# Batch norm on one core: loads cut into two transfers of 64 partitions, stores held until half of the next load has landed, and an added DRAIN on GpSimd

## The chip, the core and the metric

The kernel runs on one core of a Trainium2 chip. Time is device microseconds of one execution, from several executions of each kernel; less is better. A profile is one further execution, taken by the hardware profiler, with its own time. The engines that matter here are ScalarE (ACT in the profile), VectorE (DVE), GpSimd (POOL) and SyncE (SP), and 16 DMA engines that move bytes between the main memory (HBM) and the on-chip memory (SBUF, 128 partitions).

## What is computed

Batch normalization with given statistics: every element of `x` (32 x 256 x 128 x 128, float32, 537 MB) is scaled and shifted by two numbers that depend only on its channel.

```python
mean, var = running_mean.reshape(1, -1, 1, 1), running_var.reshape(1, -1, 1, 1)
return gamma * (x - mean) / np.sqrt(var + 1e-5) + beta
```

The output is as large as the input, so each execution reads 537 MB and writes 537 MB.

## The kernel before

The input is seen as 64 tiles (image, half of the channels), each of 128 channels on 128 partitions by 16384 elements, which is 64 KB a partition and 8 MB a tile. Three buffers of this size (`bufs`, `NBUF = 3`) take turns: tile i lies in buffer i mod 3, is loaded, changed in place and stored from there.

**Parameters.** Four small loads (L92), a transpose and a few small instructions on VectorE (L109 to L125) make `scale_t` and `shift_t`, one column for each half of the channels. This is over at 17 us.

**Loads** are issued by SP on one DMA queue. Tile 0 comes in two halves of the columns (L89 and L96), with the four small loads between them; tiles 1 and 2 as one DMA each (L98); tiles 3 to 63 as one DMA of 128 partitions each (L160), which waits on the semaphore `stored` of its buffer, that is, for the store of the tile three before. When a load has landed, its semaphore (`first` for tiles 0 to 2, `loaded` after that) has risen by 16. The helper `landed(i)` (L100) gives semaphore and value for tile i.

**Computing.** For each tile ScalarE does one ACTIVATE in place (L142, `scale * x + shift`) as soon as `landed(i)` holds. VectorE takes a part of the first and of the last tile (L131), which shortens these two. ScalarE counts its tiles in `adone`.

**Stores.** Tiles 0 to 60 are stored by GpSimd (L172), each as one DMA that waits for `adone`; the last three by ScalarE itself, in the order of its own instructions. So loads, GpSimd's stores and ScalarE's stores have a DMA queue each, and all run on the same 16 DMA engines.

**The end.** SP waits for the last stores (L177, L178). Then the block that holds the hand-written part closes (its instructions are at L73): every engine executes a DRAIN, an instruction that waits until the engine's earlier work is done, and SP waits for all of them.

Of the kernel before, what the change touches and what calls it, by code (L numbers as in the profile page):

```python
# [8 lines left out]
NBUF = 3  # L9
PAD = 936  # L10
NHEAD = 3
NTAIL = 3
# [4 lines left out]
@with_exitstack  # L17
def kernel(
    ctx: ExitStack,
    tc: tile.TileContext,  # L20
    x: bass.AP,
    gamma: bass.AP,
    beta: bass.AP,
    running_mean: bass.AP,
    running_var: bass.AP,
    out: bass.AP,
):
    nc = tc.nc
    eps = 1e-5
    f32 = mybir.dt.float32  # L30

    N, C, H, W = x.shape
    P = nc.NUM_PARTITIONS
    assert C % P == 0
    NCB = C // P
    HW = H * W
    NT = N * NCB
    B = 32
    NQ = P // B
    NE = 16  # L40
    NPAR = 4

    xr = x.rearrange("n (cb p) h w -> (n cb) p (h w)", p=P)
    outr = out.rearrange("n (cb p) h w -> (n cb) p (h w)", p=P)

    params = ctx.enter_context(tc.tile_pool(name="params", bufs=1))
    data = ctx.enter_context(tc.tile_pool(name="data", bufs=1))
    params.tile([P, PAD], f32, name="pad", tag="pad")
    bufs = [data.tile([P, HW], f32, name=f"t{s}", tag=f"t{s}") for s in range(NBUF)]
    rows = params.tile([B, NPAR * C], f32, name="rows", tag="rows")  # L50
    turned = params.tile([B, NPAR * C], f32, name="turned", tag="turned")
    par = params.tile([P, NPAR, NCB], f32, name="par", tag="par")
    eps_t = params.tile([P, 1], f32, name="eps_t", tag="eps")
    std_t = params.tile([P, NCB], f32, name="std_t", tag="std")
    rstd_t = params.tile([P, NCB], f32, name="rstd_t", tag="rstd")
    scale_t = params.tile([P, NCB], f32, name="scale_t", tag="scale")
    ms_t = params.tile([P, NCB], f32, name="ms_t", tag="ms")
    shift_t = params.tile([P, NCB], f32, name="shift_t", tag="shift")

    loaded = [tc.alloc_semaphore(f"loaded{s}") for s in range(NBUF)]
    stored = [tc.alloc_semaphore(f"stored{s}") for s in range(NBUF)]
    closed = [tc.alloc_semaphore(f"closed{s}") for s in range(NBUF)]
    early = tc.alloc_semaphore("early")
    first = [tc.alloc_semaphore(f"first{s}") for s in range(NHEAD)]
    vdone = tc.alloc_semaphore("vdone")
    adone = tc.alloc_semaphore("adone")
    fetched = tc.alloc_semaphore("fetched")
    vec = tc.alloc_semaphore("vec")  # L70
    act = tc.alloc_semaphore("act")

    with tc.tile_critical():  # L73
        count = [0]

        def step(inst, sem=None, value=None):
            if sem is not None:
                inst._wait_ge(sem, value)
            elif count[0]:
                inst._wait_ge(vec, count[0])  # L80
            inst.then_inc(vec, 1)
            count[0] += 1
            return count[0]

        left, right = slice(0, HW // 2), slice(HW // 2, HW)
        last = NT - 1


        nc.sync.dma_start(out=bufs[0][:, left], in_=xr[0][:, left]).then_inc(early, 16)  # L89
        zeroed = step(nc.vector.memset(rows[:], 0.0))  # L90
        for r, ap in enumerate((running_var, gamma, beta, running_mean)):
            inst = nc.sync.dma_start(out=rows[0:NE, r * C : (r + 1) * C], in_=ap.partition_broadcast(NE))  # L92
            if r == 0:
                inst._wait_ge(vec, zeroed)
            inst.then_inc(fetched, 16)
        nc.sync.dma_start(out=bufs[0][:, right], in_=xr[0][:, right]).then_inc(first[0], 16)  # L96
        for i in range(1, NHEAD):
            nc.sync.dma_start(out=bufs[i][:], in_=xr[i]).then_inc(first[i], 16)  # L98

        def landed(i):  # L100
            if i < NHEAD:
                return first[i], 16
            s = i % NBUF
            before = 1 if s < NHEAD else 0
            return loaded[s], 16 * (i // NBUF + 1 - before)


        step(nc.vector.memset(eps_t[:], eps))  # L108
        step(nc.vector.transpose(out=turned[:], in_=rows[:]), fetched, 16 * NPAR)  # L109
        blocks = turned.rearrange("p (rc q b) -> p rc q b", q=NQ, b=B)  # L110
        flat = par.rearrange("p r cb -> p (r cb)")
        for q in range(NQ):
            placed = step(nc.vector.tensor_copy(out=flat[q * B : (q + 1) * B], in_=blocks[:, :, q, 0]))  # L113
        var_t, gamma_t, beta_t, mean_t = (par[:, r] for r in range(NPAR))
        nc.scalar.activation(  # L115
            out=std_t[:],
            in_=var_t,
            func=mybir.ActivationFunctionType.Sqrt,
            bias=eps_t[:],
            scale=1.0,  # L120
        )._wait_ge(vec, placed).then_inc(act, 1)
        step(nc.vector.reciprocal(out=rstd_t[:], in_=std_t[:]), act, 1)  # L122
        step(nc.vector.tensor_mul(out=scale_t[:], in0=gamma_t, in1=rstd_t[:]))  # L123
        step(nc.vector.tensor_mul(out=ms_t[:], in0=mean_t, in1=scale_t[:]))  # L124
        ready = step(nc.vector.tensor_sub(out=shift_t[:], in0=beta_t, in1=ms_t[:]))  # L125
        nc.vector.wait_ge(vec, ready)
        nc.scalar.wait_ge(vec, ready)

        def vector_part(i, first_col, end):
            t, cb = bufs[i % NBUF], i % NCB  # L130
            return nc.vector.tensor_scalar(  # L131
                out=t[:, first_col:end],
                in0=t[:, first_col:end],
                scalar1=scale_t[:, cb : cb + 1],
                scalar2=shift_t[:, cb : cb + 1],
                op0=mybir.AluOpType.mult,
                op1=mybir.AluOpType.add,
            ).then_inc(vdone, 1)

        def scalar_part(i, first_col):  # L140
            t, cb = bufs[i % NBUF], i % NCB
            return nc.scalar.activation(  # L142
                out=t[:, first_col:],
                in_=t[:, first_col:],
                func=mybir.ActivationFunctionType.Identity,
                bias=shift_t[:, cb : cb + 1],
                scale=scale_t[:, cb : cb + 1],
            ).then_inc(adone, 1)


        def share(i):
            return VHEAD if i == 0 else VLAST if i == last else 0

        vector_part(0, 0, HW // 2)._wait_ge(early, 16)
        vector_part(last, 0, VLAST)._wait_ge(*landed(last))


        for i in range(NHEAD, NT):
            s = i % NBUF
            inst = nc.sync.dma_start(out=bufs[s][:], in_=xr[i])  # L160
            if i >= NBUF:
                inst._wait_ge(stored[s], 16 * (i // NBUF))
            inst.then_inc(loaded[s], 16)

        for i in range(NT):
            eng = nc.gpsimd if i < NT - NTAIL else nc.scalar
            packet = {"single_packet": True} if i < NT - NTAIL else {}
            written = (stored if i < NT - NTAIL else closed)[i % NBUF]
            scalar_part(i, share(i))._wait_ge(*landed(i))
            if i in (0, last):  # L170
                eng.wait_ge(vdone, 1 if i == 0 else 2)
            eng.dma_start(out=outr[i], in_=bufs[i % NBUF][:], **packet)._wait_ge(adone, i + 1).then_inc(  # L172
                written, 16
            )

        for s in range(NBUF):
            nc.sync.wait_ge(stored[s], 16 * ((NT - NTAIL - s + NBUF - 1) // NBUF))  # L177
            nc.sync.wait_ge(closed[s], 16)  # L178
# [30 lines left out]
```

## Time and profile before

| | |
|---|---|
| Time, median of 3 runs | 2497.66 us (2485.99 to 2506.67) |
| Profiled execution, time | 2486.73 us |
| Its span | 2485.0 us |
| ScalarE busy | 885.6 us (36%) |
| VectorE busy | 13.1 us (1%) |
| GpSimd busy | 32.7 us (1%) |
| Read from and written to HBM | 536.94 MB, 536.87 MB |
| Mean rate over the span | 432 GB/s |
| One full-tile ACTIVATE | 14.04 us |
| Idle of ScalarE that a load ended | 1555.7 us |
| Wait of SP for stores, before its loads | 2370.4 us, 61 times |

The span runs from the first to the last instruction of the profiled execution; its time is 1.7 us longer. In the rows of the profile, L142 is a line of the kernel, an arrow `out<-in` names what an instruction writes and reads, and what stands in brackets or behind "idle before" is how long the engine had waited and for what. SPq, POOLq and the like are the sequencers of the engines, which wait, issue DMAs and execute DRAINs.

### The profile page before, as it was taken

The page shows a single profiled execution, that of the slowest core. Times are in us where ns is not written, and L with a number is a line of the kernel's source. Part 1 is how long each engine was busy: PE and PEld are TensorE (multiplying, and loading weights), DVE is VectorE, ACT ScalarE, POOL GpSimd, SP SyncE. Part 2 cuts the span into 40 slices and gives each one's busy share as a digit, 9 for nine tenths or more (in the row PEclk, how much of TensorE's full clock was granted, in tenths as well). Part 3 has the DMA queues.
Part 4 walks back from the last instruction along what each step waited for, and adds up shares of the span by engine and source line. Part 5 has one row for each costly group of instructions (what it writes and reads, how often), then busy time and mean ns, then how long its engine had stood idle before and what let it go on. Part 6 is the DMA issues. An engine that isn't in the chain of part 4 may idle for free.

```text
span 2485.0 us, 274 instructions
## 1 busy us (share of the span) xinstructions
DVE 13.1 (1%) x13; ACT 885.6 (36%) x66; POOL 32.7 (1%) x65
## 2 busy tenths in 40 slices
DVE  1000000000000000000000000000000000000000
ACT  2342432423424334243342433424324244243331
POOL 0000000000000000000000000000000000000000
DMA  9999999999999999999999999999999999999998
GB/s 414 431 439 438 423 439 438 436 426 439 438 427 435 438 439 423 439 438 435 427 439 438 426 436 438 438 424 439 438 434 428 439 438 425 437 438 437 425 439 371
DMA packets 18707, 1073.84 MB, mean 432 GB/s; under 512 B 2128, under 2 KB 2192, under 8 KB 2192
## 3 DMA queue, kind: packets, MB, share of 16 engines
q1 hardware_dynamic: 9488, 536.94, 49.9%
q0 software_dynamic: 8784, 511.71, 47.5%
q10 hardware_dynamic: 432, 25.17, 2.3%
q14 instruction: 3, 0.02, 0.0%
HBM read 536.94 MB, written 536.87 MB: 432 GB/s over the span
## 4 chain that ended last, share of the span: by engine, by line
another core or an unknown queue 61%; ACT 35%; DMA 2%; issue 0%; SPq 0%; DVE 0%; ACTq 0%; DVEq 0%
ACT t L142 35%; DMA t<-in_x_dram 2%; SPq L92 0%; DVE rows L90 0%; ACTq L172 0%; SPq L96 0%; DVE eps_t L108 0%; DVEq L204 0%; SPq L73 0%
## 5 line engine op out<-in xcount | busy, mean ns | idle before, releaser
L142 ACT ACTIVATE t<-t,shift_t,scale_t 128x16384 f32<-128x16384 f32 (+1 forms) x64 | 884.0, 13813 | 1555.7 <-DMA t<-in_x_dram 1555.7
L172 POOL DMA_DIRECT2D out_dram<-t x61 | 32.5, 533 | 2314.5 <-ACT t L142 2314.5
L131 DVE TENSOR_SCALAR t<-t,scale_t,shift_t 128x8192 f32<-128x8192 f32 (+1 forms) x2 | 9.6, 4812 | 2428.0 <-DMA t<-in_x_dram 2427.9
L115 ACT ACTIVATE std_t<-par,eps_t 128x2 f32<-128x2 f32 x1 | 0.3, 295 | 13.9 <-DVE par L113 13.9
L115 ACT ACT_TABLE_LOAD x1 | 1.3, 1283 | 0.9 <-SPq L73 0.9
L109 DVE STREAM_TRANSPOSE turned<-rows 32x1024 f32<-32x1024 f32 x1 | 1.2, 1232 | 11.8 <-DMA rows<-in_running_mean_dram 11.8
L90 DVE MEMSET rows<- 32x1024 f32 x1 | 0.9, 912 | 1.2 <-SPq L73 1.2
L113 DVE COPY par<-turned 32x8 f32<-32x8 f32 x4 | 0.6, 162 | 0.1
L122 DVE RECIPROCAL rstd_t<-std_t 128x2 f32<-128x2 f32 x1 | 0.2, 166 | 0.4 <-ACT std_t L115 0.4
L124 DVE TENSOR_TENSOR ms_t<-par,scale_t 128x2 f32<-128x2 f32 x1 | 0.2, 161 | 0.0
L125 DVE TENSOR_TENSOR shift_t<-par,ms_t 128x2 f32<-128x2 f32 x1 | 0.2, 161 | 0.0
L123 DVE TENSOR_TENSOR scale_t<-par,rstd_t 128x2 f32<-128x2 f32 x1 | 0.2, 160 | 0.0
L193 POOL MEMSET const-float32-0.0<- 128x1 f32 x1 | 0.1, 98 | 0.2 <-issue 0.2
L193 POOL MEMSET const-bfloat16-1.0<- 128x1 bf16 x1 | 0.1, 101 | 0.0
L193 POOL MEMSET const-float32-1.0<- 128x1 f32 x1 | 0.1, 98 | 0.0
L193 POOL MEMSET const-uint8-127<- 128x1 uint8 x1 | 0.1, 98 | 0.0
L108 DVE MEMSET eps_t<- 128x1 f32 x1 | 0.1, 59 | 0.1
## 6 DMA issues: line engine op xcount, KB each, us to landing
t<-in_x_dram SPq DMA_DIRECT2D x2, 4096.0 KB, 15.9
t<-in_x_dram SPq DMA_DIRECT2D x63, 54.6
out_dram<-t POOLq DMA_DIRECT2D x61, 46.9
out_dram<-t ACTq DMA_DIRECT2D x3, 32.9
rows<-in_running_var_dram SPq DMA_DIRECT2D x1, 16.0 KB, 11.1
rows<-in_gamma_dram SPq DMA_DIRECT2D x1, 16.0 KB, 10.9
rows<-in_beta_dram SPq DMA_DIRECT2D x1, 16.0 KB, 10.7
rows<-in_running_mean_dram SPq DMA_DIRECT2D x1, 16.0 KB, 10.6
```

Source lines behind the costliest of these rows:

```text
L90: zeroed = step(nc.vector.memset(rows[:], 0.0))
L109: step(nc.vector.transpose(out=turned[:], in_=rows[:]), fetched, 16 * NPAR)
L113: placed = step(nc.vector.tensor_copy(out=flat[q * B : (q + 1) * B], in_=blocks[:, :, q, 0]))
L115: nc.scalar.activation(out=std_t[:], in_=var_t, func=mybir.ActivationFunctionType.Sqrt, bias=eps_t[:], scale=1.0,)._wait_ge(vec, placed).t ...
L122: step(nc.vector.reciprocal(out=rstd_t[:], in_=std_t[:]), act, 1)
L123: step(nc.vector.tensor_mul(out=scale_t[:], in0=gamma_t, in1=rstd_t[:]))
L124: step(nc.vector.tensor_mul(out=ms_t[:], in0=mean_t, in1=scale_t[:]))
L125: ready = step(nc.vector.tensor_sub(out=shift_t[:], in0=beta_t, in1=ms_t[:]))
L131: return nc.vector.tensor_scalar(out=t[:, first_col:end], in0=t[:, first_col:end], scalar1=scale_t[:, cb : cb + 1], scalar2=shift_t[:, cb ...
L142: return nc.scalar.activation(out=t[:, first_col:], in_=t[:, first_col:], func=mybir.ActivationFunctionType.Identity, bias=shift_t[:, cb : ...
L172: eng.dma_start(out=outr[i], in_=bufs[i % NBUF][:], **packet)._wait_ge(adone, i + 1).then_inc(written, 16)
L193: nc = _bacc.Bacc("TRN2", target_bir_lowering=False, num_devices=1)
```

## The change

Three things are changed.

1. From tile 1 on, a load is two DMAs, partitions 0 to 63 and partitions 64 to 127, issued by SP one after the other on the same queue. The first raises a new semaphore `lower` of its buffer, the second raises `loaded`. Only the first waits for the store three tiles before. Tile 0 is loaded as before. ScalarE and VectorE wait for both semaphores before they read a tile.
2. The store of tile i (i < 63) waits, besides `adone`, until the lower half of tile i + 1 has landed. This holds for GpSimd's stores and for ScalarE's stores of tiles 61 and 62, where the wait stands in ScalarE's own order.
3. After its last store GpSimd waits until its stores have landed, and then executes a DRAIN.

```diff
-    first = [tc.alloc_semaphore(f"first{s}") for s in range(NHEAD)]
+    lower = [tc.alloc_semaphore(f"lower{s}") for s in range(NBUF)]
+    first = tc.alloc_semaphore("first")
...
+        half = P // 2
+
+        def load(i):
+            s = i % NBUF
+            inst = nc.sync.dma_start(out=bufs[s][:half], in_=xr[i][:half])
+            if i >= NBUF:
+                inst._wait_ge(stored[s], 16 * (i // NBUF))
+            inst.then_inc(lower[s], 16)
+            nc.sync.dma_start(out=bufs[s][half:], in_=xr[i][half:]).then_inc(loaded[s], 16)
+
+        def landed(i):
+            if i == 0:
+                return first, 16
+            s = i % NBUF
+            return loaded[s], 16 * (i // NBUF + (1 if s else 0))
+
+        def half_landed(i):
+            s = i % NBUF
+            return lower[s], 16 * (i // NBUF + (1 if s else 0))
+
         for i in range(1, NHEAD):
-            nc.sync.dma_start(out=bufs[i][:], in_=xr[i]).then_inc(first[i], 16)
+            load(i)
...
         vector_part(0, 0, HW // 2)._wait_ge(early, 16)
+        nc.vector.wait_ge(*half_landed(last))
         vector_part(last, 0, VLAST)._wait_ge(*landed(last))
 
         for i in range(NHEAD, NT):
-            s = i % NBUF
-            inst = nc.sync.dma_start(out=bufs[s][:], in_=xr[i])
-            if i >= NBUF:
-                inst._wait_ge(stored[s], 16 * (i // NBUF))
-            inst.then_inc(loaded[s], 16)
+            load(i)
 
         for i in range(NT):
...
+            if i:
+                nc.scalar.wait_ge(*half_landed(i))
             scalar_part(i, share(i))._wait_ge(*landed(i))
+            if i < last:
+                eng.wait_ge(*half_landed(i + 1))
             if i in (0, last):
                 eng.wait_ge(vdone, 1 if i == 0 else 2)
             eng.dma_start(out=outr[i], in_=bufs[i % NBUF][:], **packet)._wait_ge(adone, i + 1).then_inc(
                 written, 16
             )
+
+        for s in range(NBUF):
+            nc.gpsimd.wait_ge(stored[s], 16 * ((NT - NTAIL - s + NBUF - 1) // NBUF))
+        nc.gpsimd.drain()
```

## The prediction

> **What bounds the kernel now.** I read the page first, then two stretches of the span with the busy share of the DMA engines, then the timeline of one tile, then the waits of SP, then the end. The page's DMA queues (packets, MB, share of the time of 16 engines):
>
> ```profile
> span 2485.0 us, 274 instructions
> ...
> q1 hardware_dynamic: 9488, 536.94, 49.9%
> q0 software_dynamic: 8784, 511.71, 47.5%
> q10 hardware_dynamic: 432, 25.17, 2.3%
> ```
>
> Loads (q1) and stores (q0 from GpSimd, q10 from ScalarE) together hold the 16 engines for 49.9 + 47.5 + 2.3 = 99.7% of the span, 2477.5 us of 2485.0. ScalarE is busy 36%. Two stretches, one tile in the middle and the last 9 us (after the length: busy DVE, ACT and POOL, the clock, DMA share, GB/s):
>
> ```profile
> 207.50:246.10 38.60, 0.00 (x0) 14.04 (x1) 0.53 (x1) 1.00 1.00 435
> 2476.00:2485.00 9.00, 0.00 (x0) 0.00 (x0) 0.00 (x0) 1.00 0.00 1
> ```
>
> In the middle no DMA time is free; from about 2476 on the DMA does nothing. The timeline of that tile:
>
> ```profile
> 207.50 14.04 ACT L142 ACTIVATE t<-t,shift_t,scale_t 128x16384 f32<-128x16384 f32 x1 [24.57 <-DMA t<-in_x_dram]
> 221.84 0.53 POOL L172 DMA_DIRECT2D out_dram<-t  x1 [38.08 <-ACT t L142]
> 230.00 0.33 SPq L160 DMA_DIRECT2D t<-in_x_dram  x1
> 246.28 14.04 ACT L142 ACTIVATE t<-t,shift_t,scale_t 128x16384 f32<-128x16384 f32 x1 [24.74 <-DMA t<-in_x_dram]
> ```
>
> Call the landing of a tile T (207.5). Its store is issued at T+14.3. The store before it lands at T+22.5, since that releases the load at 230.00. The next tile lands at T+38.6 to T+38.8. So the store queue is handed new work 8.2 us before it is empty, the load queue 16.3 us before. A tile is 128 rows of 64 KB each way, 8 rows an engine if they are spread evenly; 16 rows in 38.63 us is 2.414 us a row (27.1 GB/s an engine). Issue to landing, from the page:
>
> ```profile
> t<-in_x_dram SPq DMA_DIRECT2D x63, 54.6
> out_dram<-t POOLq DMA_DIRECT2D x61, 46.9
> ```
>
> 54.6 = 16.3 in the queue + 38.3; 46.9 = 8.2 + 38.7: a load and a store run side by side, each at half the rate. The end, from SP's waits and from the instructions of the kernel's closing (duration in ns: least, median, most):
>
> ```profile
> SPq L73 <- POOLq L73: 4.5, 1, 4.5
> ```
> ```profile
> L73 POOLq DRAIN  x1: 5047/5047/5047, 2479.0 to 2479.0; - x1
> ```
> ```profile
> L204 POOLq DRAIN  x3: 34/34/108, 2484.1 to 2484.7; - x3
> ```
>
> After the last byte SP waits 4.5 us more for one DRAIN of GpSimd that takes 5.05 us. Three others, with no DMA issued since the one before, take 0.03 to 0.11 us.
>
> **Halves.** 63 loads become 126, each of 64 rows. Bytes and row length stay. SP issues 63 more at 0.33 us, 20.8 us in all, on an engine that waits 2370 us for stores; the second issue of a pair goes out 0.4 us after the first, under 16.3 us of queued work: nothing. Two of the extra issues stand at the start (tiles 1 and 2), ahead of loads that wait for stores until 75 us: nothing. Each transfer posts 16 more completions of 4 bytes, 63 an engine; in the trace's packet records one takes 9 ns, so +0.6 us if none is hidden. The rows are the unknown. No transfer of the trace goes to 64 partitions. One bound is a row as now, 2.414 us; the other is two engines that write to the same part of SBUF and halve each other, 4.83 us. The nearest row in size and path, the full-tile load, is the first, and I take it; the other bound is a rival below.
>
> **The hold.** Store i now also waits for the lower half of tile i+1. With halves served one after the other that half lands at T+19.3 (half of 38.6), and ScalarE is done at T+14.04, so the store goes out at about T+19.7 instead of T+14.3: 5.4 us of the store queue's 8.2 are used, 2.8 are left. The store lands at most 5.4 us later, the load that it releases too, and that queue's cover falls from 16.3 to 10.9 us. Should the store queue run dry for a row, its engines go on with load rows at the same rate (early in the span, with loads alone, the queue moved bytes without stores too), and the row lost by one queue is won by the other. Cost 0 while either queue has rows; behind the waiting store on GpSimd stands only the next store. If both covers were gone, each tile would show a gap; that is a rival too. ScalarE's extra wait before each ACTIVATE is for a half that landed earlier: some tens of ns, in an engine with 24.6 us idle a tile.
>
> **The tail.** The last three stores stand on ScalarE, where a hold also delays the next ACTIVATE. Tile 62's activation starts at 2412.42; its store would wait until about 2412.4 + 19.3 = 2431.7 instead of going at 2426.49. The next ACTIVATE waits for its load (2449.76) anyway: nothing. The delayed store leaves more rows for the time in which the last tile is computed (2449.76 to 2456.15), when only store rows can feed the DMA. In the records the store of tile 62 lands at 2459.4, so that cover is thin now, some 3 us, and gets wider. In this profile it just suffices, so nothing is won here.
>
> **The DRAIN.** GpSimd's last store lands at 2396.4 (records). Then 5.05 us of DRAIN run beside 76 us of other traffic. If the closing DRAIN then costs what the three short ones cost, SP's 4.5 us go. Bounds: 4.5 won, or 0 if that DRAIN is long whenever GpSimd has issued DMAs, or for another reason. I take 4.5, by the three rows. What is late next is nothing: the other engines' arrivals at 2479.0.
>
> **Sum.** On the profiled execution, 2486.73: −4.5 + 0.6 + 0 = 2482.8. That execution is 10.9 us under the median of the three runs (2485.99 to 2506.67), whose excess no trace shows. A thin tail cover could be a part of it, and that part the hold would take. I leave half of the 10.9: 2488. This case alone ranges from 2478 (another 4.8 less) to 2510 (the DRAIN wins nothing and 20 us of spread as above).
>
> **Rivals.** *Collisions in the half tile (slower).* All 16 engines work on 64 partitions at a time. That few partitions do get all 16 engines the counts bear out: q1's 9488 packets are 8384 rows and pieces of rows and 69 × 16 completions, the 16-partition parameter loads with 16 too. If 64 partitions take in only half of 434 GB/s, 217 GB/s, a load row that coincides with its partner's takes 2.41 us more. Per tile an engine has 8 load rows; each that collides adds 2.41 × 64 = 154 us. It decides the sign from 0.3 rows a tile on (40 us); one is 2637, all eight 3718. For it: the engines' rows of a kind now run nearly in step, as the DMA bursts show. Against: loads need only 217 GB/s beside stores, so partners that alternate, one loading while the other stores, never collide, and an engine ahead by half a tile writes to the other half. The trace cannot settle it; 0.32, half of it under three rows a tile. [...]
>
> *The hold empties the queues (slower).* If the two halves share the engines, the lower lands with the upper at T+38.6 and the store goes out 24 us later than now. Both covers are gone: load i+2 and store i run together, end together, and the next load waits for the store's completion and its issue. Completion (DMA idle from about 2477, SP released at 2478.8) and first bytes after an issue (0.96 to about 2) are 2.5 us a tile; 61 of them are 153 us: 2636. For it: both halves stand on one queue at once. Against: one queue is served in order, as the 16.3 us of queueing show. 0.07. [...]
>
> *The DRAIN isn't shortened:* its closing copy waits as long. 2487 on the profiled execution, up to 2498. 0.07.
>
> *Faster by over 1%.* The DMA floor of 2477.5 and the ends leave 7 us; only if the before runs sit high (2507) and the hold steadies all of them at 2480 is it 1%. 0.04.
>
> **How the numbers follow.** Forecast 0.50. About 1% is what a measurement of this kernel tells from no change: 2472.7 to 2522.6. Within: 0.50 + 0.07 = 0.57; slower 0.32 + 0.07 = 0.39; faster 0.04. The range takes 2478 to 2510 (0.56 with the DRAIN rival), the empty queues (0.07) and collisions up to 2.7 rows a tile, 2482.8 + 2.7 × 154 = 2900 (0.16): 0.79.
>
> **What would show it.** Right: DMA share 1.00 in the middle, ACT landings still 38.6 us apart, GpSimd's issue near T+19.7, SP's closing wait near zero with a long GpSimd DRAIN near 2400. Collisions: DMA share 1.00 at a lower GB/s. Empty queues: share under 1.00 and landings 41 us apart. My forecast is wrong if the rate in the middle falls under 430 GB/s.

## The result, and the profile after

The changed kernel takes 3434.7 us (median of 5 runs, 3403.74 to 3455.42) against 2497.66 us before (with two runs more 2485.99 to 2520.68): 1.372 times the time, with a 95% interval of 1.364 to 1.380. The ratio is of the fast runs alone and leaves out the one of 3455.42 us, more than 1.5% above the fastest. The profiled execution took 3446.63 us, its span is 3444.9 us. The page's DMA queues (packets, MB, share of the time of 16 engines):

```profile
span 3444.9 us, 465 instructions
...
q1 hardware_dynamic: 10496, 536.94, 61.2%
q0 software_dynamic: 8784, 511.71, 36.3%
q10 hardware_dynamic: 432, 25.17, 1.7%
```

The bytes are the same, and the 16 engines are still busy 99.2% of a span that is 960 us longer. So the engines hardly wait more than before; the same rows take longer. In engine time, share times span: loads 2108 us (before 1240), stores 1309 us (before 1237), idle 28 us (before 7). The added 960 us are 868 in loads, 72 in stores and 20 in idle time. Two tiles, from landing to landing (length, busy DVE, ACT and POOL, clock, DMA share, GB/s):

```profile
1009.30:1112.93 103.63, 0.00 (x0) 28.08 (x2) 1.06 (x2) 1.00 1.00 325
```

DMA share 1.00 at 325 GB/s, where 435 GB/s went with the same share before: the sign that the prediction had named for collisions. The timeline of one tile:

```profile
1009.30 14.04 ACT L159 ACTIVATE t<-t,shift_t,scale_t 128x16384 f32<-128x16384 f32 x1 [39.11 <-DMA t<-in_x_dram]
1036.92 0.53 POOL L190 DMA_DIRECT2D out_dram<-t  x1 [50.07 <-DMA t<-in_x_dram]
1043.85 0.47 SPq L104 DMA_DIRECT2D t<-in_x_dram  x1
1044.36 1.35 SPq L108 DMA_DIRECT2D t<-in_x_dram  x1
1059.32 14.04 ACT L159 ACTIVATE t<-t,shift_t,scale_t 128x16384 f32<-128x16384 f32 x1 [35.97 <-DMA t<-in_x_dram]
```

A tile lands at 1009.30 and the next one 50.0 us later (38.6 before). GpSimd's store is released by the load's half, at T+27.6, not by ScalarE, which was done at T+14.04. The load issued at 1043.85 stands behind a load that lands at 1059.32, so the load queue is still handed work 15.5 us before it is empty. The store queue is not always so well covered. One tile earlier:

```profile
986.32 0.53 POOL L190 DMA_DIRECT2D out_dram<-t  x1 [55.11 <-DMA t<-in_x_dram]
986.33 0.47 SPq L104 DMA_DIRECT2D t<-in_x_dram  x1
```

The load at 986.33 was released by the landing of the store before, so the store at 986.32 found its queue empty. In the trace as a whole, 19 of the 60 stores that GpSimd issues after its first one go out less than 1 us before the store ahead of them lands, or after it; in the kernel before, all 60 go out at least 7.7 us ahead. The load queue has at least 6.7 us of work left at each issue. Issue to landing:

```profile
t<-in_x_dram SPq DMA_DIRECT2D x126, 63.7
out_dram<-t POOLq DMA_DIRECT2D x61, 57.5
```

In the records of single rows (64 KB, one engine), a load row has a mean of 4.14 us, a tenth of them under 2.84 and a tenth over 5.04; before, nearly all took 2.418. A store row has a mean of 2.56 us (before 2.418). The more load rows run at once, the longer they take: 3.44 us where some 8 of the 16 engines hold one while the row runs, 4.44 us at some 12 and 5.01 us at some 16. In the kernel before it is 2.42 to 2.43 us at all these counts.

The DRAIN did what was forecast. Of the closing instructions, the one of GpSimd is now

```profile
L74 POOLq DRAIN  x1: 34/34/34, 3443.7 to 3443.7; - x1
```

34 ns in place of 5047, and SP no longer waits for it. The added DRAIN has the 5047 ns now, 100 us ahead of the end, beside the last loads and stores:

```profile
L197 POOLq DRAIN  x1: 5047/5047/5047, 3342.3 to 3342.3; - x1
```

GpSimd's last store had landed before it, as in the kernel before (2396.4, the DRAIN at 2479.0), so no trace shows what the 5047 ns go into.

### The profile page after: what moved, and what is told of

It is laid out like the page before. It is cut to its first block, busy times and chain, and to the rows that moved or that the text cites. A ratio compares the mean times of both kernels' runs of the same rounds, so it can differ in the third digit from the quotient of the medians.

```text
span 3444.9 us, 465 instructions
## 1 busy us (share of the span) xinstructions
DVE 13.1 (0%) x13; ACT 885.6 (26%) x66; POOL 32.7 (1%) x65
## 4 chain that ended last, share of the span: by engine, by line
another core or an unknown queue 92%; DMA 4%; SPq 3%; ACT 0%; issue 0%; DVE 0%; ACTq 0%; DVEq 0%; POOLq 0%
DMA t<-in_x_dram 3%; SPq L108 2%; DMA out_dram<-t 1%; SPq L104 1%; ACT t L159 0%; SPq L93 0%; DVE rows L91 0%; SPq L97 0%; ACTq L190 0%; DVE eps_t L125 0%; DVEq L227 0%; ACTq L184 0%; ACTq L187 0%; POOLq L187 0%
## 6 DMA issues: line engine op xcount, KB each, us to landing
rows<-in_beta_dram SPq DMA_DIRECT2D x1, 16.0 KB, 10.9
```

## The experiments

**Moving data alone.** The first question was what a row costs when 64 partitions are loaded. This kernel issues loads, then stores, then both, in stretches with a wait between them. The first three stretches:

```diff
+        for k in range(9):
+            load(k % 3, slice(0, 128))
+        settle(nc.sync)
+        for k in range(9):
+            load(k % 3, slice(0, 64))
+        settle(nc.sync)
+        for k in range(9):
+            load(k % 3, slice(32, 96))
+        settle(nc.sync)
...
```

> Moves data only, in stretches one after the other: nothing is computed and only a part of the output is written. Nine loads each of partitions 0 to 127, 0 to 63, 32 to 95, 64 to 127, 0 to 31; then six stores each of 0 to 127, 0 to 63, 32 to 95; then eight loads of 32 to 95 beside four full stores, and eight loads of 0 to 63 beside four full stores. Theory (64 partitions on one side take half the rate): loads at 434, 217, 434, 217 and 217 GB/s, a row of 64 KB in 2.41 us where the group lies on both sides and 4.83 us where it lies on one; beside stores, loads of 32 to 95 keep 2.42 us a row and loads of 0 to 63 don't. Rival (fewer than 128 partitions are slow whichever they are): 32 to 95 as slow as 0 to 63. Stores: the trace of the kernels says nothing; as the loads if the limit holds for reads too, 434 GB/s in all three if it holds for writes only.

One window inside each stretch, in this order: loads of 0 to 127, of 0 to 63, of 32 to 95; stores of 0 to 127, of 0 to 63; loads of 32 to 95 and then of 0 to 63, both beside full stores (length, busy POOL, clock, DMA share, GB/s):

```profile
20.00:160.00 140.00, 0.00 (x0) 1.00 0.99 429
200.00:340.00 140.00, 0.00 (x0) 1.00 0.99 202
376.00:440.00 64.00, 0.00 (x0) 1.00 1.02 440
...
760.00:840.00 80.00, 1.06 (x2) 1.00 1.00 433
870.00:960.00 90.00, 1.62 (x3) 1.00 1.02 210
...
1060.00:1200.00 140.00, 1.60 (x3) 1.00 1.01 413
1240.00:1380.00 140.00, 1.06 (x2) 1.00 1.00 301
```

The DMA engines are equally busy in all of them (share 0.99 to 1.02), and the rate falls by half where the 64 partitions are 0 to 63 (202 GB/s of 429). It does not fall for 32 to 95 (440), a transfer of the same shape, size and number of rows. From the records, over whole stretches:

```
                    GB/s   row us           GB/s   row us
loads  0 to 127     431    2.43     stores  431    2.43
loads  0 to 63      204    5.12     stores  204    5.11
loads  32 to 95     429    2.43     stores  430    2.43
loads  64 to 127    204    5.12
loads  0 to 31      204    5.12
```

So it is not the number of partitions but which they are. 0 to 31 are as fast as 0 to 63 (204 GB/s both), and 32 to 95, with 32 partitions from either side of 64, have the full rate (429). Loads and stores are alike in the groups that both moved (204 and 204, 429 and 430). The theory holds for these groups, except that a row of a group on one side takes 5.12 us, somewhat more than twice 2.42 (4.84). Beside full stores, the loads of 0 to 63 have 4.36 us a row and the stores 2.55: nearly the 4.14 and 2.56 of the changed kernel. Beside full stores, the loads of 32 to 95 have 2.64 us in the mean and 2.42 in the median, so most of them are as short as undisturbed ones, but not all.

**The hold taken away.** This leaves the half-tile loads alone, with the DRAIN.

```diff
-            if i < last:
-                eng.wait_ge(*half_landed(i + 1))
```

> The changed kernel without the hold: stores wait for the ACTIVATE alone. Theory (collisions): stays at 3350 to 3500 us, load rows still about 4.1 us in the mean. Rival (the hold empties the queues): within 2% of the kernel before, about 2490 us.

It took 3282.8 us in one run, with load rows of 3.84 us. The halves carry the loss without the hold. The time lies below the expected range, and below all runs of the changed kernel, so the hold seems to cost time there too, some 164 us between the two profiled executions, as far as a single run can say. The DMA share stayed at 1.00, so with the hold rows are longer:

```profile
1000.00:1200.00 200.00, 0.00 (x0) 56.16 (x4) 2.13 (x4) 1.00 1.00 332
```

The traces show a part of the reason. Without the hold, 3 of the 60 stores found the store queue empty or within 1 us of it, with the hold 19. While store rows are missing, more engines hold load rows at once: fourteen or more for 17% of the time with the hold, 11% without. Even at equal counts rows are longer with the hold (3.44 us against 3.15 at some 8), so the rest stays open.

**Other partitions in the first transfer.** The same kernel cut so that the first transfer of a tile lies on both sides.

```diff
-            inst = nc.sync.dma_start(out=bufs[s][:half], in_=xr[i][:half])
+            inst = nc.sync.dma_start(out=bufs[s][32:96], in_=xr[i][32:96])
...
-            nc.sync.dma_start(out=bufs[s][half:], in_=xr[i][half:]).then_inc(loaded[s], 16)
+            nc.sync.dma_start(out=bufs[s][0:32], in_=xr[i][0:32]).then_inc(loaded[s], 16)
+            nc.sync.dma_start(out=bufs[s][96:128], in_=xr[i][96:128]).then_inc(loaded[s], 16)
...
```

> The changed kernel with the loads cut at other partitions: first 32 to 95, then 0 to 31, then 96 to 127, so three transfers a tile. Theory (a group of partitions that lies in both outer quarters' sides of SBUF gets the full rate, 0 to 63 alone or 64 to 127 alone half of it): 4 of 8 rows an engine don't collide; in the changed kernel 8 rows lost 1.72 us each, so 4 x 1.72 x 64 = 440 us over 2482: 2850 to 3000 us. Rival (a transfer of fewer than 128 partitions is slow whichever they are, or each transfer costs): 3440 us or more, since there are more and smaller transfers.

It took 3325.4 us in one run: faster than any run of the changed kernel although it has a transfer more, but outside both expectations. The records show why the size was off. The load rows of each tile, in order of their start, in eight groups of sixteen (mean us, means over 63 tiles):

```
middle first:    3.38  2.66  2.60  3.05 | 4.78  4.85  4.71  4.43
changed kernel:  3.92  3.98  4.02  3.59 | 4.03  4.53  4.81  4.26
```

The first four groups are mostly rows of 32 to 95, and the median of the second to fourth is 2.42 us: free, as the theory says. The other four, rows of the two outer quarters, lose more than the 1.72 us that I had carried over from the changed kernel: with 4.69 us in the mean they are not far from the 5.12 us of loads that run alone. That fits the store queue, which was empty or within 1 us of it at 38 of the 60 stores here; the engines were also idle for 2.6% of the span, which the expectation had not counted. I take the first and the fourth group to hold rows of two kinds, since they stand where the kinds change and their means (3.38 and 3.05) lie between those of the groups on either side: an estimate.

**Stores cut at 64 as well.**

```diff
...
-            eng.dma_start(out=outr[i], in_=bufs[i % NBUF][:], **packet)._wait_ge(adone, i + 1).then_inc(
-                written, 16
-            )
+            eng.dma_start(out=outr[i][:half], in_=bufs[i % NBUF][:half], **packet)._wait_ge(
+                adone, i + 1
+            ).then_inc(written, 16)
+            eng.dma_start(out=outr[i][half:], in_=bufs[i % NBUF][half:], **packet).then_inc(written, 16)
...
```

> The changed kernel with its stores cut at partition 64 too. Theory (64 partitions on one side take half the rate, reads like writes, as the stores of the data-only run did): store rows now stretch like the load rows, from 2.56 us to about 4.1; 8 x 1.6 x 64 = 820 us more, 4000 to 4600 us. Rival (only writes into SBUF collide in a mixed stream): about 3450 us as before this edit.

It took 3579.9 us in one run: between the two. ScalarE's three stores, the last of which runs alone, have 3.73 us a row (2.46 in the changed kernel), GpSimd's 2.73 (2.56). So store rows of one side do take longer, but in the mixed stream little (0.17 us). One might think that the engines, mostly in long load rows, rarely hold store rows together. The records do not bear that out: GpSimd's rows have 2.68 us where some 8 engines hold one and still only 2.89 us at some 14. The reason stays open.

**Halves of the columns.** Everything of the change is kept but the cut: two transfers of 128 partitions by half a row.

```diff
-            inst = nc.sync.dma_start(out=bufs[s][:half], in_=xr[i][:half])
+            inst = nc.sync.dma_start(out=bufs[s][:, left], in_=xr[i][:, left])
...
-            nc.sync.dma_start(out=bufs[s][half:], in_=xr[i][half:]).then_inc(loaded[s], 16)
+            nc.sync.dma_start(out=bufs[s][:, right], in_=xr[i][:, right]).then_inc(loaded[s], 16)
```

> Everything of the changed kernel stays (two transfers a load, the hold, the DRAIN), but the two transfers are halves of the columns on all 128 partitions (rows of 32 KB) instead of halves of the partitions. Theory (engines collide on the part of SBUF that 64 partitions cover): collisions go, about 434 GB/s in the middle, 2480 to 2500 us. Rival (two transfers a load, or the hold, cost the time): stays above 3000 us.

It took 2596.4 us (6 runs, 2578.4 to 2599.7), 1.039 times the kernel before (1.033 to 1.046). That lies outside both expectations, and far nearer the first: by the medians, the cut at partition 64 is 838 of the 937 us lost. But the column halves are not free either. Its page:

```profile
span 2597.9 us, 465 instructions
...
q1 hardware_dynamic: 18560, 536.94, 49.9%
q0 software_dynamic: 8784, 511.71, 47.5%
```

The shares of the queues are those of the kernel before to the digit, in a span 4.5% longer: again longer rows (a load row of 32 KB 1.265 us in the mean where 1.213 is the undisturbed one, a store row 2.525), though no transfer here lies on one side alone. And the store queue runs dry:

```profile
1001.41 0.33 SPq L102 DMA_DIRECT2D t<-in_x_dram  x1
1001.78 0.53 POOL L188 DMA_DIRECT2D out_dram<-t  x1 [39.34 <-DMA t<-in_x_dram]
```

The load was released by the landing of the store before, so the next store goes out some 0.4 us too late; at all 60 stores it is 0.3 to 6.5 us. Three further kernels and a second data-only one followed this second effect.

> The column halves (rows of 32 KB) without the hold. The column kernel with the hold was 4% slower than the kernel before, its rows 4% longer at a DMA share of 1.00. Theory A (rows of unequal length take the load and store turns of the engines out of step, and out of step they stretch): still 2570 to 2610 us. Theory B (the hold does it): 2480 to 2510 us.

Without the hold: 2566.8 us, 1.027 times the kernel before (1.022 to 1.033), just under the range of theory A. Not the hold, then, or not it alone. The store queue is still empty at 30 of the 60 stores.

> The column halves with the hold, and each store also as two transfers of half the columns, so that rows of loads and stores are equally long again (32 KB). Theory A (unequal rows): back to 2480 to 2520 us. Theory B (the hold): stays at 2570 to 2610 us.

With the stores cut by columns as well (two DMAs a store, edited as above but with `left` and `right`): 2487.57 us, and 0.9966 times the kernel before (0.9934 to 0.9997). All ten runs lie within 2487.18 to 2488.31, those of the kernel before on the same chip within 2485.59 to 2520.69. That agrees with theory A as written, but the next run speaks against its mechanism.

> Moves data only, in stretches: nothing is computed and only a part of the output is written. Ten loads beside ten stores each time, with no wait but for the buffers: full rows of both; loads by halves of the columns beside full stores; both by halves of the columns; loads and stores of partitions 32 to 95; then the column loads alone. Theory A (unequal rows): rows 2.42 us (1.21 for half a row) everywhere but in the second stretch, there about 4% more. Rival (loads of 32 KB rows are longer by themselves): the third and the last stretch stretch too.

Windows of its five stretches: full rows both ways, column loads beside full stores, column halves both ways, partitions 32 to 95 both ways, column loads alone:

```profile
60.00:380.00 320.00, 0.00 (x0) 1.00 1.00 432
440.00:680.00 240.00, 0.00 (x0) 1.00 1.01 436
850.00:1160.00 310.00, 0.00 (x0) 1.00 1.00 434
1230.00:1370.00 140.00, 0.00 (x0) 1.00 1.00 432
1420.00:1560.00 140.00, 0.00 (x0) 1.00 1.00 430
```

No stretch loses, the unequal one neither (its rows have 1.225 and 2.418 us). Unequal rows alone stretch nothing here, with both queues kept full. So theory A falls as it was stated. What the second stretch does show is that the stores alone moved 291 of its 436 GB/s, two thirds, which fits rows that take turns, one of 64 KB beside one of 32 KB. In the two kernels with unequal rows the stores may so run ahead until their queue is dry, as counted above; where both are cut it never is (9.1 us of work left at a store read in the kernel with the hold, at least 7.8 us at each store without it). That the dry queue costs the time there is a rival that no run here excludes. It can't be all, as the next run shows.

> Loads and stores by halves of the columns and the DRAIN, without the hold. With the hold all ten runs lay within 2487.2 to 2488.3 us, the runs of the kernel before within 2485.6 to 2520.7. If the hold steadies the runs: spread of more than 10 us again, median 2485 to 2500. If the equal rows do it alone: within 2 us again, at 2483 to 2488 us.

Column halves both ways but no hold: 2552.1 us, 1.021 times (1.016 to 1.026), its six runs within 6 us. So with equal rows and without the hold 2% are lost. Neither expectation holds: the hold matters by 65 us, in the median. Here the store queue was covered by at least 7.8 us at each store.

> The same kernel as the one with loads and stores by halves of the columns, with the hold and the DRAIN, once more beside the one without the hold: 2487 to 2488.5 us in all runs if its steadiness was no accident of one chip.

With the hold again, on the same chip: 2487.4 us, 0.9951 times the kernel before (0.9916 to 0.9987), all twelve runs within 2487.12 to 2487.83. The same window of the kernel without the hold:

```profile
1000.00:1200.00 200.00, 0.00 (x0) 70.20 (x5) 5.27 (x10) 1.00 1.00 422
```

and of the kernel with it:

```profile
1000.00:1200.00 200.00, 0.00 (x0) 70.20 (x5) 5.26 (x10) 1.00 1.00 434
```

In the mean, the hold leaves rows undisturbed (1.213 us for a store row and 1.215 for a load row), and without it they have 1.243 and 1.236 us. But it is not that every row stretches by 2%: without the hold 91% of the load rows and 95% of the store rows stay within 1% of 1.213 us, and the others take up to 3.4 us.

One difference in the records is how far the engines are in step. The load rows in flight, counted at many instants between 600 and 2300 us, lie between 0 and 16, one for each engine. With the hold two or fewer, or fourteen or more, are in flight 68% of the time, so the engines load together and store together; without it some 30% of the time, and each count from 0 to 16 has 3 to 9%. But other traces speak against this as the cause. The kernel before has its engines in two groups (4, 5, 11 or 12 rows in flight for 74% of the time) and undisturbed rows too, and the column loads beside whole stores without the hold have 78% at the two ends of the count and long rows all the same (1.250 and 2.471 us). Why some rows are long, and why the hold helps here but costs time beside the half-tile loads, stays open.

**The DRAIN alone.**

```diff
+        for s in range(NBUF):
+            nc.gpsimd.wait_ge(stored[s], 16 * ((NT - NTAIL - s + NBUF - 1) // NBUF))
+        nc.gpsimd.drain()
```

> The kernel before with nothing but the DRAIN added after GpSimd's last store has landed. Theory: SP's closing wait for GpSimd falls from 4.5 us to near 0, 4.5 us less on the profiled execution, about 2482 us when undisturbed. Rival (the closing DRAIN is short for a reason that lies in the halves or the hold): closing wait still 4.5 us.

Its closing DRAIN:

```profile
L73 POOLq DRAIN  x1: 34/34/34, 2495.2 to 2495.2; - x1
```

The first theory holds: 34 ns, with unsplit loads and no hold. The profiled execution is 2498.5 us nevertheless, 16 us above the 2482 expected. Its load rows had 2.443 us in the mean against 2.420, 12 us over the whole kernel; an eighth of them are more than 1% longer, the others unchanged. The other 5 us are a gap while the last tile is computed, until ScalarE issues the last store at 2474.19:

```profile
2470.00:2475.00 5.00, 2.88 (x1) 4.16 (x1) 0.00 (x0) 1.00 0.03 13
```

DMA share 0.03: the store of the tile before had landed, and nothing was left to move. The fastest of its runs, 2481.26, is 4.3 us under the fastest of the kernel before on the same chip, 2485.58. As a ratio nothing can be told: 1.0006 (0.9958 to 1.0054), under runs that spread over 33 us.

## Why the prediction was wrong

**The row of a half-tile load** is the step that failed. The prediction gave two bounds, 2.414 us as before and twice that, 4.83 us, for two engines that halve each other, and took the first for the sum, since the full-tile load was nearest in size and path. So the collisions stood in the sum with nothing. Measured: 4.14 us in the mean in the kernel, 5.12 us when loads run alone; that is 868 of the 960 us. Nearest in size and path was not nearest in the thing that counts, the partitions that are written. A full-tile load takes partitions from both sides of 64, a half-tile load from one side only, and 32 to 95 beside 0 to 63 (2.43 us a row against 5.12) shows that this is what counts, with all else equal.

**The rival of the collisions** was right about the half rate and nearly in its price: 154 us for each of the 8 rows of an engine that collides, 3718 us for all. The measured 868 us in loads are 5.6 rows at that price, or 5.0 at the 2.70 us by which a row of 0 to 63 is longer when loads run alone (5.12 us against 2.42). So the equivalent of 3 of the 8 rows escaped. That engines halve each other in pairs was the author's estimate, and no run shows pairs. The prediction had argued that partners which alternate between loading and storing escape altogether; the longer rows at more loads in flight (3.44 us at some 8, 5.01 at some 16) fit that in part, but no run tests it alone. It also read the engines as nearly in step; the records of the kernel before show two groups (4, 5, 11 or 12 load rows in flight for 74% of the time). And its range ended at 2.7 rows for no other reason than the chances.

The half rate stood in the prediction as an estimate, 217 of 434 GB/s, behind an "if": no row of the trace showed it. No row spoke against it either, and it got too little weight. The runs show 204 GB/s for loads of 0 to 63 and of 0 to 31, and 429 for 32 to 95.

**The hold at no cost** failed in two places. In the queueing, the lower half was to land at T+19.3 and to leave 2.8 us of the store queue's cover. It landed at T+27.6 in the tile above, and at 19 of 60 stores less than 1 us was left. The load queue stayed covered by at least 6.7 us, so the rival in which both queues run empty and the DMA share falls under 1.00 is refuted. In the price, the prediction let a dry store queue cost nothing, because the engines "go on with load rows at the same rate". Half-tile loads alone go at 204 GB/s where full-tile loads go at 431. The hold moved the time by some 164 us upwards beside half-tile loads, and by 65 us downwards beside column halves both ways, where no queue ran dry. No step of the prediction had either term. (Its price for empty queues also adds up a little higher than it says: 1.8 us from the end of the DMA to SP's release and some 1.0 us from issue to first bytes are 2.8 us a tile, not 2.5.)

**The halves' other costs** were small, as forecast. Column halves both ways have even more transfers, and the fastest run with them, 2487.12 us, is 5.9 us above the fastest with the DRAIN alone, 2481.26 us on another chip.

**The DRAIN** was right: 4.5 us forecast, a wait of 4.5 us gone from the end, 4.3 us between the fastest runs of the kernels with and without the DRAIN alone. Beside a loss of 937 us it decided nothing.

**The spread of the runs.** The prediction left half of the 10.9 us between the profiled execution and the median to a thin tail cover. The trace of the kernel with the DRAIN alone shows that source and a larger one: a gap of 5 us ahead of the last store, and load rows 0.023 us longer in the mean over the whole execution, 12 us in all.

## What to carry to other kernels

A DMA share of 1.00 says that the engines are busy, not that they move bytes at their rate: it went with 435 GB/s in the kernel before and with 325 in the changed one. Read the GB/s beside it, and the time of one row (2.42 us and 4.14). When a transfer has to be cut, try first to cut it along the row, with all 128 partitions in each piece, and to cut the transfers that run beside it alike (that took 0.995 to 1.02 times the kernel before, the halves of the partitions 1.37; with whole stores the column halves still lost 3 to 4%); if 64 partitions must do, measure 32 to 95 before 0 to 63 (429 GB/s against 204). And where an unseen cost decides the sign, a short kernel that only moves data can settle it in one run. When a wait is added before a store, ask not only whether a queue stays busy, but what the engines move while the other queue is dry (half-tile loads alone 204 GB/s, full-tile loads 431).

## What the runs showed of the hardware that I had not expected

- Stores, which read SBUF, lose half their rate with the partitions as loads do: 204 GB/s for 0 to 63, 430 for 32 to 95.
- A load row of 0 to 63 takes 5.12 us when loads run alone, 6% more than twice the 2.42 us of the kernel before.
- With the bytes, the transfers' partitions and the DMA share unchanged, the mean row was 2 to 4% longer for a whole execution: with whole stores and the hold 1.265 us for a load row of 32 KB, and with column halves both ways 1.243 us for a store row without the hold against 1.213 with it. In the latter it comes from a minority of rows that take up to 3.4 us, and makes 2552.1 us against 2487.4 by a wait that stops no queue. The cause is open.
- The version with column halves both ways, the hold and the DRAIN is the steadiest: its 22 runs on two chips lie within 1.2 us, those of the kernel before within 35 us. Its medians are 0.3 to 0.5% below those of the kernel before, which is no clear gain: the fastest runs of the kernel before (2485.6 us) are faster than all 22.
